# Row operations of two block inverses from VectorE to GpSimd, modulation rows from the recurrence to the projections

## The chip, the cores and the metric

The kernel runs on one core of a Trainium2 chip. The metric is the device time of one launch in microseconds. The engines are TensorE (PE in the profile, its weight loads PEld), VectorE (DVE), ScalarE (ACT), GpSimd (POOL) and the queue that issues most loads (SP).

## What is computed

Two blocks follow each other on 512 positions of width 1024, in float32. The first is modulated by a condition c, mixes the positions with a gated convolution and with a linear recurrence in both directions (after 256 positions of context), and ends in a convolutional feed-forward part. The second block (a gated linear recurrence, windowed attention, a gated feed-forward part) is not touched by the change. Cut to what matters:

```python
mod = silu(c) @ ada_w + ada_b                      # six parts of 1024: sh1, sc1, g1, sh2, sc2, g2
hx  = modulate(rms_norm(x, norm1_g), sh1, sc1)     # and the same for ctx
cb, cc, cx, r, k, v, w_lo, a_lo, g_lo = split_proj(hx @ w_in)
def step(S, inp):                                  # per head, 64 x 64, forward and reverse
    r_t, w_t, kk_t, b_t, v_t, k_t = inp
    sa = einsum("bhvk,bhk->bhv", S, kk_t)
    S = S * w_t - sa[..., None] * b_t + v_t[..., None] * k_t
    return S, einsum("bhvk,bhk->bhv", S, r_t)
y_conv = cb * shortconv1d(cc * cx, conv_a_w)
x = x + g1 * (concatenate([y_conv, y_rwkv]) @ w_out)
x = x + g2 * conv_ffn(modulate(rms_norm(x, norm2_g), sh2, sc2))
```

## The kernel before

**Products.** Large products run as three products of rounded parts (mm3): high by high, high by low, low by high. A weight piece of 128 x 512 is loaded (w), rounded by ScalarE (whi) and the rest is formed by VectorE, wlo = w - whi (split, L178 to L182; its argument `eng` can name another engine). wsplit does this for the pieces of a tile.

**Projections** (proj, some 60 to 261 us). 26 tiles of w_in come in a fixed order of code: 24, 16 to 19, 12 to 15, then the preparation of the first pair of heads, the products for v, tile 25, and for j = 0 to 3 the tiles 4+j, 8+j and j, with steps of the second pair's preparation between. A tile's two pieces are k0 = 0 and k0 = 4.

**Recurrence** (rwkv, 261 to 545 us). It goes through four pairs of heads, called pair 0 to 3 here (j in the code), in four stages, each of twelve groups g of one chunk per direction. A group is a chain of small products c and copies by ScalarE (RU, S); VectorE masks the scores psc into AS. Ahead of its stage each pair needs prep(j): low-rank products pl, decay sums cs (scan), b, KB and KR for each direction, products pa into AK, and then inverse(j), which inverts the 24 triangular 64 x 64 blocks: transpose to U, 31 steps of two operations on 128 partitions (tmp = U x X, X = X - tmp) with n*w = (31-k)(k+1) elements per partition, at most 256, two transposes F1 and F2, and two rounds of small products, pt and po. VectorE does the 62 operations of each inverse:

```python
tv = tmp[:, 0:n * w].rearrange("p (a b) -> p a b", b=w)
nc.vector.tensor_tensor(out=tv, in0=U[...].to_broadcast(...), in1=X[...].to_broadcast(...), op=ALU.mult)
nc.vector.tensor_tensor(out=X[:, k + 1:32, 0:w], in0=X[:, k + 1:32, 0:w], in1=tv, op=ALU.subtract)
```

inverse(0) runs beside the projections, inverse(1) in stage 0, inverse(2) in stage 1 and inverse(3) in stage 2. At the end of a stage GpSimd forms vt, rk and ys, and grs for the stage's normalisation.

**Modulation, second part** (ada12, L525 to L542). The parts of mod from g1 on come from 32 rows: each is a load of 128 x 1024 values (adaw) and one VectorE operation, a product with cb summed along the row (L539). The results go into self.mod, which is first read after the recurrence. The rows are taken from `todo`, the list of side work from which each group takes steps; after stage 1 it holds splits(), ada12() and first(), the last of which loads and splits the first two pieces of w_out, whose products px follow stage 3.

**Order.** The framework's scheduler orders each engine's stream ahead of time, by priorities that stage() sets (base + PK x g for the chain, plus PF for side work) and by its own model of durations. On the chip each engine takes its stream in order and waits for semaphores.

Of the kernel before, what the change touches and what calls it, by code (L numbers as in the profile page):

```python
# [10 lines left out]
F32 = mybir.dt.float32  # L11
# [3 lines left out]
ALU = mybir.AluOpType  # L15
# [3 lines left out]
P = 128  # L19
# [103 lines left out]
class K:  # L123
# [175 lines left out]
    def proj(self):  # L299
        nc, A, r1, p0 = self.nc, self.A, self.r1, self.p0  # L300
# [27 lines left out]
        acc = self.t3("acc", "sg")  # L328
# [13 lines left out]
        hc = [t[:, i, :] for tag, n in (("KB10", 6), ("KB11", 6), ("KR10", 5)) for t in [self.pp.tile([P, n, NC_], F32R, tag=tag, name="hc", bufs=1)] for i in range(n)]  # L342
        hhi = [[None] * KD, hc[:KD]]
        hlo = [[None] * KD, hc[KD:2 * KD]]
        piece = lambda u, k0: self.wsplit(A["win"][u][:, k0:k0 + 4], 4, P)
        ahead = {(24, k0): piece(24, k0) for k0 in (0, 4)}
        G = self.pp.tile([P, KD, 2], F32, tag="bo", name="G", bufs=2)
        for kc in range(KD):
# [12 lines left out]
                    nc.vector.scalar_tensor_tensor(out=hlo[i][kc], in0=xT[i][kc], scalar=sh, in1=hhi[i][kc].bitcast(F32), op0=ALU.add, op1=ALU.subtract)  # L361
        nc.gpsimd.memset(self.AK, 0.0)

        def tile_of(u, x=True, c=True):
            ws = [ahead.pop((u, k0), None) or piece(u, k0) for k0 in (0, 4)]
            w = lambda k: ws[k // 4](k % 4)
            out = []
            for on, i, n in ((x, 0, NX), (c, 1, NC_)):
                if on:
                    pm = self.psmm(n)  # L370
                    self.mm3(pm, [(*w(k), hhi[i][k], hlo[i][k]) for k in range(KD)])
                    out.append(pm)
            return out
# [80 lines left out]
        for j in range(4):  # L454
            t = self.zx[j]
            pcc, = tile_of(4 + j, c=False)
            nc.scalar.activation(out=t, in_=pcc, func=AF.Copy)
            pcx, = tile_of(8 + j, c=False)
            u = r1.tile([P, NX + 2], F32, tag="u", name="u", bufs=1)
            nc.gpsimd.memset(u[:, 0:1], 0.0)  # L460
            nc.gpsimd.memset(u[:, NX + 1:NX + 2], 0.0)
            nc.vector.tensor_tensor(out=u[:, 1:NX + 1], in0=t, in1=pcx, op=ALU.mult)
            nc.scalar.activation(out=t, in_=u[:, 0:NX], func=AF.Copy, scale=self.v("conva", j))
            for i in (1, 2):
                nc.vector.scalar_tensor_tensor(out=t, in0=u[:, i:i + NX], scalar=self.v("conva", 4 * i + j), in1=t, op0=ALU.mult, op1=ALU.add)
            pcb, = tile_of(j, c=False)
            nc.vector.tensor_tensor(out=t, in0=t, in1=pcb, op=ALU.mult)
            for _ in range(self.RC):
                next(self.todo, None)


    def consts(self):
# [5 lines left out]
    def rwkv(self, es, ep):  # L478
# [9 lines left out]
        for j in range(4):  # L488
            if j < 2:
                todo = chain(todo, self.prep(j + 2))  # L490
            gn = self.stage(j, self.S[j], todo, self.RB[j], gn)
            if j == 1:
                for _ in todo:
                    pass
                ep.close()
                self.wp = self.pool(es, "wp", side="right")
                self.mmbufs, self.axbufs, self.wbufs, self.wsbufs = 6, 2, 3, 4
                pa = self.pool(self.ea, "pmix", side="right")
                self.ahi = [pa.tile([P, NX], F32R, name=f"ahi{i}") for i in range(8)]
                self.alo = [pa.tile([P, NX], F32R, name=f"alo{i}") for i in range(8)]  # L500
                todo = chain(self.splits(), self.ada12(), self.first())
                self.e3 = es.enter_context(ExitStack())
                self.psa = self.psum(self.e3, "psa", side="right")
        for _ in todo:
# [20 lines left out]
    def ada12(self):  # L525

        nc, wp = self.nc, self.wp
        tags = [("w", self.wbufs), ("whi", self.wsbufs), ("wlo", self.wsbufs)]
        cb, sb = (wp.tile([P, 1024], F32, tag=tags[i][0], name="cb", bufs=tags[i][1]) for i in (1, 2))
        nc.sync.dma_start(out=cb, in_=self.A["cb"])  # L530
        nc.scalar.activation(out=sb, in_=cb, func=AF.Tanh, scale=0.5)
        nc.vector.tensor_scalar(out=sb, in0=sb, scalar1=0.5, scalar2=0.5, op0=ALU.mult, op1=ALU.add)
# [1 line left out]
        acc = wp.tile([P, 32], F32, name="adacc")  # L534
        for n in range(32):
            yield
            w, t = (wp.tile([P, 1024], F32, tag=tags[i][0], name="adaw", bufs=tags[i][1]) for i in (0, 2))
            nc.sync.dma_start(out=w, in_=self.A["adat"][n])
            nc.vector.scalar_tensor_tensor(out=t, in0=w, scalar=1.0, in1=cb, op0=ALU.mult, op1=ALU.mult, accum_out=acc[:, n:n + 1])  # L539
            if n in (7, 23, 31):  # L540
                a = 0 if n == 7 else 8 if n == 23 else 24
                nc.vector.tensor_tensor(out=self.mod[:, 16 + a:17 + n, 0], in0=acc[:, a:n + 1], in1=self.v("ada_b", 16 + a, n + 1 - a), op=ALU.add)  # L542
# [107 lines left out]
    def inverse(self, j):  # L650
# [12 lines left out]
        nc.vector.transpose(out=U, in_=AK[:, :, 0:32].rearrange("p n i -> p i n"))  # L663
        nc.gpsimd.memset(X, 0.0)
        nc.gpsimd.memset(X.rearrange("p a b -> p (a b)")[:, ::33], 1.0)
        for k in range(31):
            if k % 4 == 0:
                yield
            n, w = 31 - k, k + 1
            tv = tmp[:, 0:n * w].rearrange("p (a b) -> p a b", b=w)  # L670
            nc.vector.tensor_tensor(out=tv, in0=U[:, k + 1:32, k:k + 1].to_broadcast([P, n, w]), in1=X[:, k:k + 1, 0:w].to_broadcast([P, n, w]), op=ALU.mult)
            nc.vector.tensor_tensor(out=X[:, k + 1:32, 0:w], in0=X[:, k + 1:32, 0:w], in1=tv, op=ALU.subtract)
        F1, F2 = big("F1"), big("F2")
        nc.vector.transpose(out=F1.rearrange("p n i -> p i n"), in_=X)
        nc.vector.transpose(out=F2.rearrange("p n j -> p j n"), in_=X.rearrange("p i j -> p j i"))
# [721 lines left out]
```

## Time and profile before

| | |
|---|---|
| Median of three runs | 1590.84 us (1588.16 to 1595.9) |
| The profiled execution | 1591.34 us |
| Its span in the trace | 1589.5 us |
| TensorE busy | 1498.6 us, 94% |
| VectorE busy | 999.9 us, 63% |
| ScalarE busy | 632.7 us, 40% |
| GpSimd busy | 121.7 us, 8% |
| Projections / recurrence | about 60 to 261 / 261 to 545 us |

Times of a trace count from the start of the span; what the execution has beyond its span is 1.8 us. A matmul's busy time overlaps that of the next one. An idle time ahead of an instruction is put down to the event that ended it.

### The profile page before, as it was taken

How to read it: one execution, taken by the hardware profiler on the slowest of the kernel's cores; microseconds unless marked ns; L12 is line 12 of the kernel's file. 1: busy time of each engine (PE TensorE's matmuls, PEld its weight loads, DVE VectorE, ACT ScalarE, POOL GpSimd, SP SyncE). 2: the span in 40 equal slices, each digit the busy share in tenths (PEclk: the TensorE clock that was granted, in tenths of full speed). 3: DMA queues.
4: the chain of work that ended last, by engine and by line, in shares of the span. 5: the costliest groups of instructions: out<-in, count | busy, mean ns of one | idle time of the engine just before them, and what ended most of it. 6: DMA issues, size and time to landing. Idle time of an engine off the chain costs nothing. (4 is left out here: it accounts for less than half of the span.)

```text
span 1589.5 us, 28932 instructions
## 1 busy us (share of the span) xinstructions
PE 1498.6 (94%) x12062; PEld 1228.9 (77%) x12062; DVE 999.9 (63%) x1691; ACT 632.7 (40%) x1258; POOL 121.7 (8%) x141
## 2 busy tenths in 40 slices
PE   4899999989888999999999997999999999999998
PEld 2777787877777898888888875887677888888886
DVE  3436765777867669888863448588965555554221
ACT  3524343555453334333332325335554333333122
POOL 1111001020110000000000004121200000000000
PEclk9999898989999999999999998999999999999999
DMA  9243321010057613223323322211112222233221
GB/s 339 87 156 104 100 89 60 4 45 5 15 197 258 214 40 119 94 93 101 98 83 100 96 93 70 80 54 54 36 59 93 93 93 93 93 94 106 93 92 54
DMA packets 62179, 152.83 MB, mean 96 GB/s; under 512 B 12640, under 2 KB 14432, under 8 KB 62048
## 3 DMA queue, kind: packets, MB, share of 16 engines
q1 hardware_dynamic: 58016, 143.95, 27.9%
q10 hardware_dynamic: 4032, 7.04, 1.3%
q8 instruction: 94, 1.54, 0.4%
q14 instruction: 37, 0.30, 0.1%
HBM read 143.10 MB, written 7.86 MB: 95 GB/s over the span
## 5 line engine op out<-in xcount | busy, mean ns | idle before, releaser
L181 ACT ACTIVATE whi<-w 128x1024 fp32r<-128x1024 f32 (+2 forms) x220 | 208.7, 950 | 448.2 <-PE pm L170 333.3
L182 DVE TENSOR_TENSOR wlo<-w,whi 128x1024 fp32r<-128x1024 f32 (+2 forms) x212 | 229.9, 1086 | 201.3 <-ACT whi L181 195.3
L169 PE MATMUL pm<-ahi,whi 128*128 128x512 f32 (+1 forms) x624 | 236.4, 379 | 3.0 <-DVE sh L1080 2.6
L170 PE MATMUL pm<-alo,whi 128*128 128x512 f32 (+1 forms) x624 | 234.8, 376 | 0.0
L171 PE MATMUL pm<-ahi,wlo 128*128 128x512 f32 (+1 forms) x624 | 234.0, 375 | 0.0
L170 PE MATMUL pm<-al,whi 128*128 128x512 f32 x352 | 139.7, 397 | 0.0
L169 PE MATMUL pm<-ah,whi 128*128 128x512 f32 x352 | 139.2, 395 | 0.0
L171 PE MATMUL pm<-ah,wlo 128*128 128x512 f32 x352 | 139.2, 395 | 0.0
L169 PEld LDWEIGHTS pm<-ahi,whi 128*128 128x128 f32 x624 | 117.6, 189 | 24.2 <-ACT sh L1095 3.0
L171 PEld LDWEIGHTS pm<-ahi,wlo 128*128 128x128 f32 x624 | 117.6, 188 | 20.6 <-issue 0.7
L170 PEld LDWEIGHTS pm<-alo,whi 128*128 128x128 f32 x624 | 117.7, 189 | 20.3 <-issue 0.7
L953 DVE SCALAR_TENSOR_TENSOR cv<-pm,vec,cv 128x441 f32<-128x441 f32 (+2 forms) x176 | 121.1, 693 | 4.1
L170 PEld LDWEIGHTS pm<-al,whi 128*128 128x128 f32 x352 | 66.2, 188 | 16.1 <-issue 0.2
L171 PEld LDWEIGHTS pm<-ah,wlo 128*128 128x128 f32 x352 | 66.2, 188 | 16.1 <-issue 0.2
L169 PEld LDWEIGHTS pm<-ah,whi 128*128 128x128 f32 x352 | 66.2, 188 | 16.0
L171 PE MATMUL pm<-hhi,wlo 128*128 128x512 f32 x176 | 70.8, 402 | 2.7 <-DVE wlo L182 2.7
L169 PE MATMUL pm<-hhi,whi 128*128 128x512 f32 x176 | 71.4, 406 | 0.2 <-ACT whi L181 0.2
L170 PE MATMUL pm<-hlo,whi 128*128 128x512 f32 x176 | 70.6, 401 | 0.0
L169 PE MATMUL pd<-whi,gh 128*128 128x512 f32 x176 | 69.5, 395 | 0.0
L169 PE MATMUL pm<-hh,whi 128*128 128x512 f32 x176 | 69.3, 394 | 0.0
L170 PE MATMUL pm<-hl,whi 128*128 128x512 f32 x176 | 69.3, 394 | 0.0
L171 PE MATMUL pm<-hh,wlo 128*128 128x512 f32 x176 | 69.3, 394 | 0.0
(397 smaller groups left out, 3073.6 us busy)
## 6 DMA issues: line engine op xcount, KB each, us to landing
w<-in_fup SPq DMA_DIRECT2D x44, 512.0 KB, 3.7
adaw<-in_adat SPq DMA_DIRECT2D x32, 512.0 KB, 4.6
w<-in_win SPq DMA_DIRECT2D x44, 256.0 KB, 2.9
w<-in_wg SPq DMA_DIRECT2D x22, 512.0 KB, 3.6
w<-in_wu SPq DMA_DIRECT2D x22, 512.0 KB, 3.6
w<-in_wd SPq DMA_DIRECT2D x22, 512.0 KB, 3.7
w<-in_win SPq DMA_DIRECT2D x18, 512.0 KB, 3.5
w<-in_wout SPq DMA_DIRECT2D x16, 512.0 KB, 3.8
```

Of the source, the lines that this page charges most:

```text
L169: nc.tensor.matmul(out, lh, rh, start=(first and i == 0), stop=False)
L170: nc.tensor.matmul(out, lh, rl, start=False, stop=False)
L171: nc.tensor.matmul(out, ll, rh, start=False, stop=(last and i == n - 1))
L181: self.nc.scalar.activation(out=hi, in_=src, func=AF.Copy)
L182: (eng or self.nc.vector).tensor_tensor(out=lo, in0=src, in1=hi.bitcast(F32), op=ALU.subtract)
L953: nc.vector.scalar_tensor_tensor(out=o, in0=p[:, ro[0] + dr:ro[1] + dr, co[0] + dc:co[1] + dc], scalar=w(i), in1=o, op0=ALU.mult, op1=ALU.add)
```

## The change

It has three parts. (1) The row operations of the inverses of pairs 2 and 3 are issued on GpSimd instead of VectorE. (2) The 32 modulation rows are taken in proj: each tile takes one row for 12 <= u < 25 and two otherwise, from two row buffers of their own, and the product is written over the loaded row; todo after stage 1 holds splits() and first() alone. (3) For the tiles 25 and 0 to 11, the second piece's low part is formed by GpSimd. Lines below L363 move down by seven to ten; L671 and L672 are L681 and L682 in the new kernel, the modulation row L539 is L548, pt L701.

```diff
-        piece = lambda u, k0: self.wsplit(A["win"][u][:, k0:k0 + 4], 4, P)
+        piece = lambda u, k0: self.wsplit(A["win"][u][:, k0:k0 + 4], 4, P, eng=nc.gpsimd if k0 and not 12 <= u < 25 else None)
...
+        ada = self.ada12()
+        def rows(n):
+            for _ in range(n):
+                next(ada, None)
         def tile_of(u, x=True, c=True):
+            rows(1 if 12 <= u < 25 else 2)
             ws = [ahead.pop((u, k0), None) or piece(u, k0) for k0 in (0, 4)]
...
             for _ in range(self.RC):
                 next(self.todo, None)
+        for _ in ada:
+            pass
...
-                todo = chain(self.splits(), self.ada12(), self.first())
+                todo = chain(self.splits(), self.first())
...
-        tags = [("w", self.wbufs), ("whi", self.wsbufs), ("wlo", self.wsbufs)]
-        cb, sb = (wp.tile([P, 1024], F32, tag=tags[i][0], name="cb", bufs=tags[i][1]) for i in (1, 2))
+        row = lambda name: wp.tile([P, 1024], F32, tag="row", name=name, bufs=2)
+        cb, sb = wp.tile([P, 1024], F32, name="cb"), row("sb")
...
-            w, t = (wp.tile([P, 1024], F32, tag=tags[i][0], name="adaw", bufs=tags[i][1]) for i in (0, 2))
+            w = row("adaw")
             nc.sync.dma_start(out=w, in_=self.A["adat"][n])
-            nc.vector.scalar_tensor_tensor(out=t, in0=w, scalar=1.0, in1=cb, op0=ALU.mult, op1=ALU.mult, accum_out=acc[:, n:n + 1])
+            nc.vector.scalar_tensor_tensor(out=w, in0=w, scalar=1.0, in1=cb, op0=ALU.mult, op1=ALU.mult, accum_out=acc[:, n:n + 1])
...
+        e = nc.vector if j < 2 else nc.gpsimd
         for k in range(31):
...
-            nc.vector.tensor_tensor(out=tv, in0=U[:, k + 1:32, k:k + 1].to_broadcast([P, n, w]), ...
-            nc.vector.tensor_tensor(out=X[:, k + 1:32, 0:w], in0=X[:, k + 1:32, 0:w], in1=tv, op=ALU.subtract)
+            e.tensor_tensor(out=tv, in0=U[:, k + 1:32, k:k + 1].to_broadcast([P, n, w]), ...
+            e.tensor_tensor(out=X[:, k + 1:32, 0:w], in0=X[:, k + 1:32, 0:w], in1=tv, op=ALU.subtract)
```

Three places of the built order. First TensorE, stage 1, around the products pt of the inverse of pair 2; the c rows are the chain's products, c_2377 and c_2378 its two directions. Before, about the chain's tenth group:

```order
L638 MATMUL c_2377<-RU_2372,zx 64x64 x2
L638 MATMUL pkt<-cst,KB_1646 64x64 x2
L638 MATMUL c_2378<-vt,AS_2369 64x64 x2
L638 MATMUL c_2378<-S_2376,KR_1649 64x64
L691 MATMUL pt<-F_3309,AK 32x32 x24
L638 MATMUL c_2377<-vt,kbt 64x64 x2
L638 MATMUL c_2377<-S_2375,cst 64x64 x2
L638 MATMUL c_2377<-RU_2372,kbt 64x64
L638 MATMUL pa<-KR_86,KB_84 64x64 x10
L691 MATMUL pt<-F_3309,AK 32x32 x24
```

After, where c_2483 and c_2484 are the two directions:

```order
L647 MATMUL c_2483<-vt,kbt 64x64 x2
L647 MATMUL c_2483<-S_2481,cst 64x64 x2
L647 MATMUL c_2483<-RU_2478,kbt 64x64 x2
L647 MATMUL c_2483<-vt,AS_2473 64x64
L701 MATMUL pt<-F_3415,AK 32x32 x24
L647 MATMUL c_2483<-vt,AS_2473 64x64
L647 MATMUL c_2483<-S_2481,KR_1680 64x64 x2
L647 MATMUL c_2484<-RU_2480,zx 64x64 x2
L647 MATMUL pkt<-cst,KB_1678 64x64 x2
L647 MATMUL pa<-KR_86,KB_84 64x64 x9
L701 MATMUL pt<-F_3415,AK 32x32 x24
```

These products now stand about the sixth group, four groups earlier; those of pair 3 move in the same way from behind the eighth group of stage 2 to its third.

Second VectorE, projections, the end of the inverse of pair 0. Before:

```order
L671 TENSOR_TENSOR tmp<-U,X 128x87
L672 TENSOR_TENSOR X<-X,tmp 128x3x29
L671 TENSOR_TENSOR tmp<-U,X 128x60
L672 TENSOR_TENSOR X<-X,tmp 128x2x30
L671 TENSOR_TENSOR tmp<-U,X 128x31
L672 TENSOR_TENSOR X<-X,tmp 128x31
L674 STREAM_TRANSPOSE F_1294<-X 128x32x32
L675 STREAM_TRANSPOSE F_1295<-X 128x32x32
L192 COPY XT_83<-F_1294 128x768
L192 COPY XT_83<-F_1295 128x768
```

After:

```order
L682 TENSOR_TENSOR X<-X,tmp 128x5x27
L190 TENSOR_SCALAR sg<-sg,cst 128x12x64
L681 TENSOR_TENSOR tmp<-U,X 128x112
L600 SCALAR_TENSOR_TENSOR cs<-cst,sg 128x780
L682 TENSOR_TENSOR X<-X,tmp 128x4x28
L681 TENSOR_TENSOR tmp<-U,X 128x87
L619 SCALAR_TENSOR_TENSOR b_1924<-ta,kk 128x768
L682 TENSOR_TENSOR X<-X,tmp 128x3x29
L620 SCALAR_TENSOR_TENSOR KB_1678<-b_1924,sg 128x12x64
L681 TENSOR_TENSOR tmp<-U,X 128x60
L627 TENSOR_TENSOR KR_1680<-kk,cs 128x256
L682 TENSOR_TENSOR X<-X,tmp 128x2x30
```

The first operations of pair 1's prep (sg, cs, b, KB, KR) have moved between the last row operations, and a low part of the tiles stands there; further up, four modulation rows (L548) stand among the row operations of the same inverse, and 25 ahead of it.

Third VectorE, stage 1, the transposes F of the inverse of pair 2 and what follows. Before:

```order
L671 TENSOR_TENSOR tmp<-U,X 128x31
L672 TENSOR_TENSOR X<-X,tmp 128x31
L674 STREAM_TRANSPOSE F_3308<-X 128x32x32
L675 STREAM_TRANSPOSE F_3309<-X 128x32x32
L192 COPY XT_2364<-F_3308 128x768
L192 COPY XT_2364<-F_3309 128x768
L731 COPY_PREDICATED AS_2367<-cst,psc 128x384
L731 COPY_PREDICATED AS_2370<-cst,psc 128x384
L731 COPY_PREDICATED AS_2365<-cst,psc 128x2x64
L190 TENSOR_SCALAR sg<-sg,cst 128x12x64
```

After, with the row operations gone to GpSimd:

```order
L741 COPY_PREDICATED AS_2473<-cst,psc 128x384
L741 COPY_PREDICATED AS_2476<-cst,psc 128x384
L684 STREAM_TRANSPOSE F_3414<-X 128x32x32
L685 STREAM_TRANSPOSE F_3415<-X 128x32x32
L192 COPY XT_2470<-F_3414 128x768
L192 COPY XT_2470<-F_3415 128x768
L741 COPY_PREDICATED AS_2471<-cst,psc 128x384
L741 COPY_PREDICATED AS_2474<-cst,psc 128x384
L190 TENSOR_SCALAR sg<-sg,cst 128x12x64
L602 SCALAR_TENSOR_TENSOR cs<-cst,sg 128x780
```

The rest of pair 3's prep (sg, the scan of its second direction, b) still follows the transposes F, and no row operation stands ahead of them on this engine. On TensorE the pa products of pair 3's second direction, which need it, still follow pt. The first products px, which stood behind stage 3, now begin in stage 2's last group.

## Rows read from the trace of the kernel before

**Rows 1.** The page's list of engines: busy us (share of span) x instructions.

```profile
PE 1498.6 (94%) x12062; PEld 1228.9 (77%) x12062; DVE 999.9 (63%) x1691; ACT 632.7 (40%) x1258; POOL 121.7 (8%) x141
```

**Rows 2.** Stretches: us, busy us of PE, PEld, DVE, ACT, POOL, PEclk, DMA share, GB/s.

```profile
152.00:187.00 35.00, 31.19 (x173) 24.88 (x172) 33.17 (x77) 9.91 (x17) 2.62 (x4) 0.99 0.39 112
187.00:200.00 13.00, 12.65 (x216) 10.43 (x211) 3.18 (x5) 7.31 (x15) 1.57 (x4) 0.62 0.20 63
465.00:500.00 35.00, 31.49 (x770) 27.04 (x768) 27.04 (x50) 15.88 (x66) 3.20 (x3) 1.00 0.74 247
500.00:520.00 20.00, 16.34 (x350) 14.34 (x350) 14.50 (x26) 7.94 (x32) 1.04 (x1) 0.86 0.80 272
```

**Rows 3.** Waits, 250 to 560 us: engine, line, waited for: us, times, longest.

```profile
PE pt L691 <- DVE F L675: 2.9, 3, 1.3
PE c L638 <- DVE AS L731: 5.9, 6, 1.5
PEld c L638 <- ACT RU L759: 8.3, 18, 2.8
```

**Rows 4.** Timeline of DVE: start us, us, engine, line, operation, shapes [idle before <-releaser].

```profile
184.25 1.88 DVE L675 STREAM_TRANSPOSE F<-X 128x1024 f32<-128x1024 f32 x1
331.42 0.29 DVE L671 TENSOR_TENSOR tmp<-U,X 128x31 f32<-128x31 f32 x1
376.78 1.95 DVE L675 STREAM_TRANSPOSE F<-X 128x1024 f32<-128x1024 f32 x1
398.43 1.94 DVE L663 STREAM_TRANSPOSE U<-AK 128x1024 f32<-128x1024 f32 x1 [2.10 <-POOL AK L660]
```

**Rows 5.** Timeline of ACT (S) and POOL (vt), recurrence, in order of time.

```profile
366.23 0.31 ACT L769 ACTIVATE S<-c,pc 128x64 f32<-128x64 f32 x1 [0.96 <-PE c L638]
400.02 1.04 POOL L789 TENSOR_TENSOR vt<-vt,bo 128x512 f32<-128x512 f32 x1 [0.39 <-PE c L638]
411.41 0.31 ACT L769 ACTIVATE S<-c,pc 128x64 f32<-128x64 f32 x1 [0.58 <-PE c L638]
432.28 0.31 ACT L769 ACTIVATE S<-c,pc 128x64 f32<-128x64 f32 x1 [0.96 <-PE c L638]
464.29 1.04 POOL L789 TENSOR_TENSOR vt<-vt,bo 128x512 f32<-128x512 f32 x1 [23.34 <-issue]
517.17 1.04 POOL L789 TENSOR_TENSOR vt<-vt,bo 128x512 f32<-128x512 f32 x1 [38.74 <-PE c L638]
```

**Rows 6.** Groups, DVE, 331 to 376 us: shapes xcount | busy us, mean ns | idle.

```profile
L672 DVE TENSOR_TENSOR X<-X,tmp 128x31 f32<-128x31 f32 (+15 forms) x31 | 11.5, 371 | 0.7
```

**Rows 7.** Groups of POOL by shape, whole span, same columns.

```profile
L823 POOL TENSOR_TENSOR grs<-gv,mhalf 128x8 f32<-128x8 f32 x4 | 6.6, 1648 | 26.2 <-DVE gv L820 16.0 <-DMA adaw<-in_adat 10.2
L359 POOL TENSOR_TENSOR hc<-KB,hc 128x256 fp32r<-128x256 f32 x8 | 6.6, 832 | 14.8 <-ACT KB L358 14.8
L789 POOL TENSOR_TENSOR vt<-vt,bo 128x512 f32<-128x512 f32 x4 | 4.2, 1042 | 62.5 <-PE c L638 39.1 <-issue 23.3
L808 POOL TENSOR_TENSOR ys<-Y 128x512 f32<-128x512 f32 x3 | 3.8, 1262 | 0.0
L601 POOL COPY pc<-cs 128x12 f32<-128x12 f32 x8 | 3.0, 372 | 92.1 <-ACT cs L597 92.1
```

**Rows 8.** Timeline of DVE and POOL at the third inverse's start.

```profile
331.62 1.26 POOL L563 TENSOR_TENSOR rk<-rt,kt 128x512 f32<-128x512 f32 x1
331.74 1.21 DVE L672 TENSOR_TENSOR X<-X,tmp 128x31 f32<-128x31 f32 x1
```

**Rows 9.** Timeline of DVE: one modulation row, stage 2.

```profile
451.91 1.23 DVE L539 SCALAR_TENSOR_TENSOR adaw<-adaw,cb 128x1024 f32<-128x1024 f32 x1
```

**Rows 10.** Groups of PE, 519 to 545 us: first of three such.

```profile
L169 PE MATMUL px<-ahi,whi 128*128 128x512 f32 x16 | 7.4, 476 | 1.3 <-ACT ahi L181 1.3
```

**Rows 11.** Timeline of DVE: prep of pair 3, second direction.

```profile
388.82 1.78 DVE L593 TENSOR_TENSOR_SCAN cs<-cst,sg 128x780 f32<-128x780 f32 x1
391.04 0.95 DVE L610 SCALAR_TENSOR_TENSOR b<-ta,kk 128x768 f32<-128x768 f32 x1
```

More of the change, by code (lines that the diff above doesn't have):

```diff
@@ L670, in inverse @@
             tv = tmp[:, 0:n * w].rearrange("p (a b) -> p a b", b=w)
-            nc.vector.tensor_tensor(out=tv, in0=U[:, k + 1:32, k:k + 1].to_broadcast([P, n, w]), in1=X[:, k:k + 1, 0:w].to_broadcast([P, n, w]), op=ALU.mult)
-            nc.vector.tensor_tensor(out=X[:, k + 1:32, 0:w], in0=X[:, k + 1:32, 0:w], in1=tv, op=ALU.subtract)
+            e.tensor_tensor(out=tv, in0=U[:, k + 1:32, k:k + 1].to_broadcast([P, n, w]), in1=X[:, k:k + 1, 0:w].to_broadcast([P, n, w]), op=ALU.mult)
+            e.tensor_tensor(out=X[:, k + 1:32, 0:w], in0=X[:, k + 1:32, 0:w], in1=tv, op=ALU.subtract)
         F1, F2 = big("F1"), big("F2")
```

## The prediction

> **What bounds the kernel now.** The list of engines gives TensorE 1498.6 of 1589.5 us [rows 1], so the first question of any stretch is whether TensorE works or waits there. The table of stretches answers it. The change touches two places. Late in the projections (152 to 187 us) TensorE and VectorE are both nearly full, 31.19 and 33.17 of 35 us, and right after it, at 187 to 200, the granted clock is 0.62, the lower of TensorE's two levels for most of the stretch [rows 2]. In the recurrence (261 to 545 us) TensorE waits in small pieces: in the last stage, 465 to 520 us, it works 31.49 of 35 and 16.34 of 20 us, 7.2 us idle [rows 2]. The list of waits says for whom: the two inverses there cost TensorE only 2.9 us in three pieces at pt, VectorE's AS copies 5.9 us, ScalarE's RU 8.3 us [rows 3]. So VectorE's row operations are long but almost hidden; what an edit can win in the recurrence is a few us of AS waits, and the holes.
>
> The timeline shows how the inverse of pair 2 lies: its first row operation at 331.42, its second F transpose from 376.78, so ready at 378.73, and then 19.7 us until the U of pair 3 starts at 398.43 [rows 4]. Those 19.7 us are a chain that starts at pt: pt and po, then the low-rank products, sg, scan, b, KB, KR of pair 3's second direction, pa, and AK. In the changed order the same work still stands behind pt on TensorE and behind F on VectorE. Stages 1 and 2 end at 400.02 and 464.29, where vt is written [rows 5]. ScalarE's S rows place pt's new positions: half-way through the sixth of stage 1's twelve groups (TensorE there at 366) and in the third group of stage 2 (411) [rows 5].
>
> **Row operations on GpSimd.** Each of the two inverses gives 62 operations, 2 x 5456 elements per partition. VectorE did the second half of each pair in 11.5 us for 31, so about 23 us for 62 [rows 6]. The trace has no such small operation on GpSimd. The nearest rows: a subtraction of 256 elements takes 0.832 us, an addition of 512 1.262, one with a broadcast operand 1.042, a copy of 12 elements 0.372 [rows 7]. From 256 to 512 that is 1.68 ns an element over a fixed 0.40 us, and the copy of 12 says the same of the fixed part. So 62 x 0.40 = 24.8, 5456 x 1.68 = 9.2 for the subtractions, 5456 x (1042 - 400)/512 = 6.8 for the broadcast products: 41 us. No operation has more than 256 elements, so 62 x 0.832 = 51.5 us is an upper end; VectorE's own 23 us is the lower end that I work with, 18 us if GpSimd's small operations cost still less. I take 41, since both rows near the small sizes agree on the fixed part.
>
> Inverse of pair 2: GpSimd is free after vt at about 331.7. 41 us of its own; rk, ys, grs and pc stand in between, 1.26 + 1.26 + 1.65 + 0.37 = 4.5 us [rows 7]; and 4 us for collisions (0 to 8). For these: at 331.74 a 31-element VectorE operation took 1.21 us while GpSimd's rk ran from 331.62 [rows 8], where its twin at 331.42 took 0.29 [rows 4]. So the two engines do exclude each other; no row shows GpSimd as the one that waits, but none shows it working for long beside VectorE, whose other two-input work there is some 8 us. Then two F transposes, 3.9 us: ready at 385.1, where TensorE stands before pt since 366. A new wait of 19 us. From this place to the end of stage 1 TensorE had 400 - 366 = 34 us of work, 1.3 of it the old pt wait: stage 1 ends at 417.8.
>
> The Trainium skill, "SBUF — State Buffer", "SBUF: two separate sides", calls the shared port pair an exclusive lock, in which whichever of a VectorE operation with two SBUF inputs and a GpSimd operation starts first blocks the other for the whole instruction; rows 8 agree for one direction. By the rule in both directions the collisions are at their upper end and the sum would be 6 us higher, by the rows alone 6 us lower.
>
> Inverse of pair 3: U starts 19.7 us after 385.1, at 404.8, and takes 2. Then 41 us, vt, ys and grs in between 4, collisions 2, F 3.9: ready at 457.7. TensorE comes to pt at 417.8 + 11 = 428.8: a second wait, 29 us. Left of stage 2 behind this place are 464.3 - 411 = 53.3 us, less the old pt wait, RU's 2.8 (ScalarE's tanh of cb is gone from there) and some 2 of AS: 47. Stage 2 ends at 504.7, 40.4 later than before. VectorE is freed of 46 us here, but nobody waits for that: the AS waits that it ends are 5.9 us in all [rows 3] and disappear into the longer ones.
>
> **Modulation rows out of stages 2 and 3, first wout products in.** A row costs VectorE 1.23 us [rows 9] and a 512 KB load. Stage 3 ran from 464.29 to 517.17, 4.4 us for each of twelve groups, against (432.28 - 411.41)/5 = 4.17 from the third to the eighth group of stage 2, ahead of the rows [rows 5]: -3. The 48 products px stood behind stage 3; three groups like the one of 7.4 us overlap in pairs, some 10.5 us [rows 10], and now stand from stage 2's last group on. They fit into holes that measured 7.2 us: -7 (0 to -10).
>
> **Modulation rows and low parts in the projections.** 25 of the 32 rows stand ahead of the inverse of pair 0, in front of work with which VectorE has room, and their loads meet a DMA share of 0.39, where 0.80 is carried at 500 us [rows 2]: nothing for these, 1.5 for VectorE being later at pa. Inside this inverse, where VectorE has 1.8 us free, there now stand four rows, 4.9, and the head of pair 1's prep: the scan 1.78, sg and three more at most like b, 0.95, and a third of one [rows 11], 5.9 together. Three low parts go, each with half a row's elements, 1.8. Sum +9 until F. GpSimd's low parts at 1.3 us can hold a VectorE operation as in rows 8: 0 to 5, taken as 2. About 2 us more TensorE work stands ahead of pt. So pt, which TensorE waited for until 186.13 [rows 4], stands 11 us later and finds 2 of them filled, and TensorE, otherwise full, waits out the rest; with the 1.5 that is +10 (4 to 17). The end 4 is that the rows fall into gaps; 17 is all collisions and a second stretch at the lower clock like that of 187 to 200.
>
> **Sum**: 40.4 - 3 - 7 + 10 = +40 against the profiled execution of 1591.3, which is 0.5 above the median of 1590.84. Forecast 1631, its own range 1612 to 1650 (5 us more or less of each GpSimd series is 10 in the end, since the second series starts from the end of the first).
>
> **Rivals.** *GpSimd's small operations cost as much as its 256-element one.* 51.5 us each: F of pair 2 at 395.6, U of pair 3 at 415.3, F at 478.7, stage 2 to 525.7, sum +61: 1653. For it: the operations have two- and three-dimensional patterns with short rows, the rows of GpSimd are mostly long runs; against it, the copy of 12 at 0.372. *About the same.* At VectorE's price, 23 us, F of pair 2 is ready before TensorE's 366, U of pair 3 at about 386 and F at 418, stage 2 ends at 465.5, and -3, -7 and +10 cancel: 1592. It needs 0.37 us an operation, just the fixed part. *Faster.* 18 us (0.29 us an operation): stage 2 ends at 460.5, and the projections give only +4 because the rows fall into gaps: 1591 - 4 - 10 + 4 = 1581. It decides at under some 20 us a series together with a projections term under 5. For it: the rows hold no two-operand operation of GpSimd under 256 elements but the powers; against it, 18 us over 62 operations leaves nothing beside 0.29 us each, and the 12-element copy alone takes 0.372. That the change does not do what it says is out: the order shows 124 row operations on GpSimd.
>
> **How the numbers follow.** About 0.5%, 8 us, is what a measurement can tell from no change. Forecast 0.55, dear operations 0.20, about the same 0.14, faster 0.11. The range 1586 to 1658 leaves out most of the faster case and the upper part of the dear one. Slower by more than 0.5%: 0.75, within 0.14, faster 0.11.
>
> **What would show it.** Right: GpSimd's row operations at a mean of 0.6 to 0.75 us, some 40 to 46 us from first to last; waits of TensorE at pt for F of about 19 and 29 us; in the projections a wait of about 10 us ahead of pt near 190 to 200; modulation rows all before 215 us; px inside stage 3. Wrong: a mean under 0.4 us, pt waits of a few us, or stage 2 ending near 465. If the waits are there but stage 2 ends much before 500, the work behind pt was shorter than read; if the second wait is no longer than the first, U of pair 3 did not hang on pt.

## The result

The changed kernel takes 1631.95 us (median of four runs, 1625.93 to 1637.68) against 1589.5 (the median of four runs of the kernel before, one more than in the table above): a ratio of 1.0262, 95% interval 1.0212 to 1.0312. The forecast was 1631. The profiled execution took 1631.23 us with a span of 1629.4, 39.9 more than the span before.

The list of engines of the page after, to be read against [rows 1]: TensorE's work is the same, VectorE lost 39.5 us, GpSimd gained 93, and TensorE's idle time grew from 90.9 to 126.3 us.

```profile
PE 1503.1 (92%) x12062; PEld 1235.6 (76%) x12062; DVE 960.4 (59%) x1554; ACT 633.9 (39%) x1258; POOL 214.5 (13%) x278
```

Where the 39.9 us lie is read from GpSimd's vt, which is written when a stage's last chunk is done (stages 0, 2 and 3; that of stage 1 stands behind other work in GpSimd's queue and tells nothing). The vt of stage 0 before, and the timeline after, to be read against it and [rows 5]:

```profile
330.62 1.04 POOL L789 TENSOR_TENSOR vt<-vt,bo 128x512 f32<-128x512 f32 x1
```

```profile
341.69 1.04 POOL L799 TENSOR_TENSOR vt<-vt,bo 128x512 f32<-128x512 f32 x1 [0.30 <-PE c L647]
449.21 1.04 POOL L799 TENSOR_TENSOR vt<-vt,bo 128x512 f32<-128x512 f32 x1
517.98 1.04 POOL L799 TENSOR_TENSOR vt<-vt,bo 128x512 f32<-128x512 f32 x1 [46.94 <-issue]
568.19 1.04 POOL L799 TENSOR_TENSOR vt<-vt,bo 128x512 f32<-128x512 f32 x1 [42.91 <-PE c L647]
```

| Part of the span | Before | After | Difference | Term of the sum |
|---|---|---|---|---|
| to the end of stage 0 | 330.6 | 341.7 | +11.1 | +10 |
| stages 1 and 2 | 133.7 | 176.3 | +42.6 | +40.4 |
| stage 3 | 52.9 | 50.2 | -2.7 | -3 |
| behind stage 3 | 1072.3 | 1061.2 | -11.1 | -7 |

In the changed kernel without its row operations (e4 below) stages 1 and 2 last 136.3 us, so 40.0 of the 42.6 come with the row operations. TensorE's busy time there is 126.25 us after and 121.24 in e4, at mean granted clocks of 0.78 and 0.97. So some 35 us of the 40 are idle time, and 5 are the same kind of work done at a lower clock, a term that the forecast did not have.

TensorE's waits after, 330 to 520 us (engine, line, waited for: us in all, times, longest), and the table of stretches of the recurrence (columns as in [rows 2]):

```profile
PE pt L701 <- DVE F L685: 22.6, 2, 13.6
PE pv L647 <- POOL vt L799: 15.8, 2, 15.5
PE pa L647 <- DVE KB L620: 7.4, 1, 7.4
```

```profile
350.00:380.00 30.00, 22.27 (x401) 19.04 (x398) 13.69 (x16) 12.74 (x39) 27.54 (x36) 0.74 0.05 15
380.00:400.00 20.00, 6.55 (x161) 6.19 (x165) 5.01 (x5) 3.46 (x9) 10.23 (x24) 0.57 0.00 1
400.00:450.00 50.00, 34.03 (x818) 29.10 (x818) 14.18 (x19) 20.84 (x71) 26.50 (x47) 0.81 0.01 4
450.00:480.00 30.00, 19.93 (x498) 18.82 (x499) 10.43 (x16) 10.97 (x33) 15.25 (x28) 0.64 0.20 67
```

From 350 to 400 us GpSimd is the fullest engine. Between 380 and 400 TensorE works 6.55 of 20 us at a granted clock of 0.57, and from 400 to 480 it works about two thirds of the time. Four waits make up 45.4 us. The timeline of TensorE shows them in order, each with the idle time ahead of it:

```profile
368.69 0.37 PE L647 MATMUL pa<-KR,KB 64*64 64x64 f32 x1 [7.38 <-DVE KB L620]
393.45 1.49 PE L701 MATMUL pt<-F,AK 32*32 32x32 f32 x48 [13.56 <-DVE F L685]
450.31 0.79 PE L647 MATMUL pv<-cst,vt 64*64 64x64 f32 x9 [15.50 <-POOL vt L799]
468.50 1.49 PE L701 MATMUL pt<-F,AK 32*32 32x32 f32 x48 [8.99 <-DVE F L685]
```

Two of the four have another name than the wait for F that was forecast, but the same source. The first: GpSimd's grs stands in the middle of the row operations; VectorE's yc waits 7.3 us for it, and b, KR and KB of pair 3, for which TensorE's pa waits, are queued behind yc on VectorE. GpSimd's and VectorE's timeline:

```profile
362.34 1.66 POOL L833 TENSOR_TENSOR grs<-gv,mhalf 128x8 f32<-128x8 f32 x1
```

```profile
364.03 1.12 DVE L835 TENSOR_TENSOR yc<-yc,grs 128x512 f32<-128x512 f32 x1 [7.34 <-POOL grs L833]
365.07 1.43 DVE L619 SCALAR_TENSOR_TENSOR b<-ta,kk 128x768 f32<-128x768 f32 x1
367.20 1.43 DVE L620 SCALAR_TENSOR_TENSOR KB<-b,sg 128x768 f32<-128x768 f32 x1
```

The third wait: vt of stage 1 stands behind 41 row operations of pair 3, so that TensorE's pv, placed early in stage 2, waits until 450.31.

The series themselves, first and last row operation of either, one operation of 192 elements in both and the largest, and then the second F and the U around the second series (GpSimd's, then VectorE's timeline):

```profile
342.69 0.25 POOL L681 TENSOR_TENSOR tmp<-U,X 128x31 f32<-128x31 f32 x1
353.39 1.94 POOL L682 TENSOR_TENSOR X<-X,tmp 128x192 f32<-128x192 f32 x1
389.45 0.25 POOL L682 TENSOR_TENSOR X<-X,tmp 128x31 f32<-128x31 f32 x1
423.33 0.26 POOL L681 TENSOR_TENSOR tmp<-U,X 128x31 f32<-128x31 f32 x1 [0.91 <-DVE U L672]
430.64 0.59 POOL L682 TENSOR_TENSOR X<-X,tmp 128x192 f32<-128x192 f32 x1
442.02 0.73 POOL L682 TENSOR_TENSOR X<-X,tmp 128x256 f32<-128x256 f32 x1
464.48 0.25 POOL L682 TENSOR_TENSOR X<-X,tmp 128x31 f32<-128x31 f32 x1
```

```profile
391.50 1.89 DVE L685 STREAM_TRANSPOSE F<-X 128x1024 f32<-128x1024 f32 x1
421.23 1.96 DVE L672 STREAM_TRANSPOSE U<-AK 128x1024 f32<-128x1024 f32 x1 [1.64 <-POOL AK L669]
466.54 1.92 DVE L685 STREAM_TRANSPOSE F<-X 128x1024 f32<-128x1024 f32 x1
```

The first lasts 47.0 us, 5.2 of them other work (rk 1.26, ys 1.27, grs 1.66, pc 0.92, a memset 0.12); the second 41.4, less vt, ys and grs, 4.0: 37.4 us of its own, against 41.8 in the first. In the second nearly nothing of VectorE stands in the way. The 4.4 us of difference are read as collisions: the operations that grew in the first series stand beside VectorE's two-input operations, like that of 353.39 beside the scan (last section).

In the projections the wait has another name as well. TensorE does not come to pt first; it waits for a weight's high part on ScalarE (ScalarE's, then TensorE's timeline, and VectorE's second F of pair 0):

```profile
196.73 0.84 ACT L605 ACTIVATE sg<-cs 128x768 f32<-128x768 f32 x1 [3.71 <-DVE cs L600]
197.61 0.85 ACT L606 ACTIVATE cs<-cs 128x780 f32<-128x780 f32 x1
198.37 0.61 ACT L181 ACTIVATE whi<-w 128x512 fp32r<-128x512 f32 x1
```

```profile
199.03 0.79 PE L169 MATMUL pm<-hhi,whi 128*128 128x512 f32 x1 [6.74 <-ACT whi L181]
```

```profile
205.07 2.13 DVE L685 STREAM_TRANSPOSE F<-X 128x1024 f32<-128x1024 f32 x1
```

ScalarE's exponential needs VectorE's scan, which stands between the last row operations of pair 0 and starts at 194.84; whi stands behind it in ScalarE's queue.

### The profile page after: what moved, and what is told of

It reads as the page before. It is cut to its first block, busy times and chain, and to the rows that moved or that the text cites. A ratio compares the mean times of both kernels' runs of the same rounds, so it can differ in the third digit from the quotient of the medians.

```text
span 1629.4 us, 28921 instructions
## 1 busy us (share of the span) xinstructions
PE 1503.1 (92%) x12062; PEld 1235.6 (76%) x12062; DVE 960.4 (59%) x1554; ACT 633.9 (39%) x1258; POOL 214.5 (13%) x278
## 5 line engine op out<-in xcount | busy, mean ns | idle before, releaser
L182 DVE TENSOR_TENSOR wlo<-w,whi 128x1024 fp32r<-128x1024 f32 (+2 forms) x199 | 220.7, 1110 | 169.6 <-ACT whi L181 167.7
L169 PEld LDWEIGHTS pm<-ah,whi 128*128 128x128 f32 x352 | 66.1, 188 | 15.5
L741 DVE COPY_PREDICATED AS<-cst,psc 128x384 f32<-128x384 int32 (+1 forms) x48 | 23.3, 490 | 79.6 <-PE psc L647 79.3
L170 PE MATMUL pd<-wlo,gh 128*128 128x512 f32 x176 | 69.5, 395 | 0.0
L171 PE MATMUL pd<-whi,gl 128*128 128x512 f32 x176 | 69.5, 395 | 0.0
```

The costliest lines, as they stand in the source:

```text
L169: nc.tensor.matmul(out, lh, rh, start=(first and i == 0), stop=False)
L170: nc.tensor.matmul(out, lh, rl, start=False, stop=False)
L171: nc.tensor.matmul(out, ll, rh, start=False, stop=(last and i == n - 1))
L182: (eng or self.nc.vector).tensor_tensor(out=lo, in0=src, in1=hi.bitcast(F32), op=ALU.subtract)
L741: nc.vector.copy_predicated(A[:, :, 0:N], m.unsqueeze(1).to_broadcast([P, 2, N]), ps)
```

## The experiments

Ratios are to the kernel before, with 95% intervals, each against runs on the same chip. "Stages 1, 2" is the time from vt of stage 0 to vt of stage 2 in the run's trace: 133.7 us before, 176.3 after.

| Run | Ratio | Interval | Median us | Stages 1, 2 |
|---|---|---|---|---|
| row operations alone (e1) | 1.0266 | 1.0230 to 1.0303 | 1631.54 | 175.4 |
| modulation rows alone (e2) | 1.0007 | 0.9988 to 1.0026 | 1589.97 | 137.3 |
| changed, without row operations (e4) | 1.0013 | 0.9996 to 1.0030 | 1590.32 | 136.3 |
| changed, without low parts (e5) | 1.0245 | 1.0218 to 1.0272 | 1627.92 | 176.9 |
| vt and ys on VectorE (e6) | 1.0245 | 1.0220 to 1.0271 | 1624.42 | 171.5 |
| pair 3 alone on GpSimd (e7) | 1.0117 | 1.0072 to 1.0161 | 1608.22 | 156.3 |
| pair 2 alone on GpSimd (e8) | 1.0106 | 1.0084 to 1.0128 | 1602.52 | 154.7 |
| both on GpSimd, pt late (e9c) | 1.0233 | 1.0200 to 1.0266 | 1622.51 | 167.2 |
| pair 2 alone, pt late (e9) | 1.0060 | 1.0036 to 1.0084 | 1598.46 | 147.8 |
| products twice (e10) | 1.0403 | 1.0379 to 1.0428 | 1650.02 | 202.0 |
| wout ahead of the rows (e11) | 1.0037 | 1.0021 to 1.0052 | 1594.75 | 137.9 |
| all rows early (e12) | 1.0120 | 1.0099 to 1.0141 | 1607.79 | 137.9 |

### Which part costs the time

The row operations alone, on the kernel before:

```diff
+        e = nc.vector if j < 2 else nc.gpsimd
         for k in range(31):
...
-            nc.vector.tensor_tensor(out=tv, ...
-            nc.vector.tensor_tensor(out=X[:, k + 1:32, 0:w], ...
+            e.tensor_tensor(out=tv, ...
+            e.tensor_tensor(out=X[:, k + 1:32, 0:w], ...
```

> The first part alone: the kernel before with the row operations of the inverses of pairs 2 and 3 on GpSimd, modulation rows and low parts where they were. Theory (the GpSimd series are late and TensorE waits for each): the projections end as before, GpSimd's series last 41 to 47 us each, TensorE waits some 21 us for the first and some 24 us for the second, the end comes 35 to 45 us later than before, 1625 to 1635 us. Rival (the loss of the changed kernel sits in the projections and in collisions with the moved rows): under 1605 us.

The modulation rows alone (the changed kernel with `e = nc.vector` and without `eng=` in piece), and the changed kernel without its row operations (`e = nc.vector` alone):

> The second part alone: modulation rows in the projections, row operations and low parts on VectorE as before. Theory: the projections lose 7 to 11 us, and the recurrence and the first wout products gain 12 to 16, so 1582 to 1590 us. Rival (the first wout products move because VectorE is free of row operations, not because the rows are gone): no gain behind the projections, 1596 to 1602 us.

> The changed kernel without its first part: row operations of all inverses on VectorE, modulation rows and half of the low parts as changed. Theory: within 3 us of the second part alone, a little slower because GpSimd's low parts of 1.3 us hold VectorE at a few places: 1584 to 1592 us. Rival (half of the low parts on GpSimd free VectorE where it is full): 3 to 6 us faster than the second part alone.

The changed kernel without its low parts:

```diff
-        piece = lambda u, k0: self.wsplit(..., 4, P, eng=nc.gpsimd if k0 and not 12 <= u < 25 else None)
+        piece = lambda u, k0: self.wsplit(..., 4, P)
```

> The changed kernel without its third part: all low parts on VectorE. Theory (the low parts matter little): within 3 us of the changed kernel, 1627 to 1634 us. Rival (they cost the projections most of their 11 us): 1621 to 1626 us.

The row operations alone measure 1.0266, the whole change 1.0262: the first part is the whole loss. The other two parts together are 1.0013, no difference that can be told from none. For the second part alone the theory's gain is not there: 1589.97 is the upper end of its range, with a median of 1588.81 before on that chip. Its trace does show the two halves, a later end of stage 3 (520.94 against 517.17) and 11 us less behind it (1061.1 against 1072.3), but the execution that was profiled, 1583.77, is near the low end of its ten runs (1583.71 to 1595.08). Of the third part nothing can be measured in either pair (e2 against e4, e5 against the changed kernel). TensorE's longest waits of e1 in 330 to 600 us are those of the changed kernel, with rows and low parts where they were:

```profile
PE pt L692 <- DVE F L676: 22.8, 2, 13.8
PE pv L638 <- POOL vt L790: 16.5, 4, 15.5
PE pa L638 <- DVE KB L611: 8.8, 1, 8.8
```

### Is vt's place in GpSimd's queue the cause

The wait of 15.5 us for vt was not forecast, so vt and ys were given to VectorE:

```diff
-        nc.gpsimd.tensor_tensor(out=bv, in0=bv, in1=wide(bo), op=ALU.mult)
+        nc.vector.tensor_tensor(out=bv, in0=bv, in1=wide(bo), op=ALU.mult)
...
-        (nc.vector if j == 3 else nc.gpsimd).tensor_tensor(out=ys, ...
+        nc.vector.tensor_tensor(out=ys, ...
```

> The changed kernel with vt and ys of the stages' normalisation on VectorE instead of GpSimd, so that they no longer stand behind GpSimd's row operations; grs stays. Theory (the end of GpSimd's second series ends the wait, the wait for vt lies inside it): the 15.5 us wait at pv goes, the wait at pt for F grows from 9 to some 20 us, and only GpSimd's 2.3 us and a little more are won: 1626 to 1631 us. Rival (vt's place in GpSimd's queue is itself what is late): 1614 to 1620 us.

TensorE's waits of this run, 330 to 600 us:

```profile
PE pt L701 <- DVE F L685: 35.5, 2, 22.4
PE pa L647 <- DVE KB L620: 13.0, 1, 13.0
```

The wait for vt is gone, and that for F grew from 9.0 to 22.4: what ended the wait before was the series, and vt lay inside it. The wait for KB grew from 7.4 to 13.0, behind grs once more: VectorE comes to yc earlier, and yc waits 11.8 us for grs, which kept its place in the middle of the series. Stages 1 and 2 fell by 4.8 us, the time by 1.0262 - 1.0245, some 3 us (the intervals overlap). By its waits that is the theory's case. The median of 1624.42 lies between the two ranges, but on a chip on which the kernel before takes 1586.4; the ratio, put on 1589.5, gives 1628. No run here takes grs off GpSimd.

### Do the two series add up or compound

Pair 2 alone and pair 3 alone on GpSimd (`e = nc.gpsimd if j == 2 else nc.vector`, and `e = nc.vector if j < 3 else nc.gpsimd`):

> The changed kernel with the row operations of pair 2 alone on GpSimd, those of pair 3 on VectorE. Theory (each series costs its own wait, and the second starts from the first's end): the waits at pa and pt of stage 1 stay, 7 and 14 us, those of stage 2 are gone; pair 3's pt stands in the sixth group of stage 2 and VectorE's series is ready about there: 1606 to 1616 us. Rival (TensorE's second wait only takes over the first's delay, one series costs as much as two): 1625 to 1632 us.

> The changed kernel with the row operations of pair 3 alone on GpSimd, those of pair 2 on VectorE. In the built order pair 3's pt stands in the sixth group of stage 2. Theory (together the two cost more than their sum, since the second starts from the first's end; the loss of both is 2.6%, that of pair 2 alone 1.1%): U of pair 3 some 15 us earlier than in the changed kernel, F ready 49 us after it, a wait of 15 to 20 us, ratio 1.007 to 1.012. Rival (the second series alone causes what pair 2 alone doesn't): 1.015 or more.

TensorE's waits of e8 and of e7, 330 to 600 us:

```profile
PE pt L701 <- DVE F L685: 14.7, 2, 13.6
PE pa L647 <- DVE KB L620: 7.4, 1, 7.4
```

```profile
PE pt L701 <- DVE F L685: 15.0, 2, 14.5
PE c L647 <- DVE AS L741: 7.1, 2, 6.1
```

Against the changed kernel without row operations (136.3 us), stages 1 and 2 are 18.4 us longer with pair 2, 20.0 with pair 3 and 40.0 with both. So in the traces the two add up, within 2 us, and e7's "together the two cost more than their sum" is not borne out there. The medians (0.9% and 1.0% above e4, both together 2.5%) would leave room for some 8 us more, but cannot show them, with an interval of 0.9% on e7. Of e7's forecasts, the ratio of 1.0117 is inside the range and the wait of 14.5 us just under it. In e7 pair 3's U starts at 409.57, counted from stage 0's end 10 us earlier than in the changed kernel, so the first series does push the second; but pt then stands three groups later in the order than with both, and behind F are 39.8 us of stage 2 instead of 49.5. The 6.1 us wait for AS in e7 has grs in it once more: VectorE's yc (424.82) waits 6.39 us for it, and AS is queued behind yc.

Each product twice, which makes either series some 18 us longer (first to last row operation 65.0 and 59.3 us against 47.0 and 41.4):

```diff
-            e.tensor_tensor(out=tv, ...
+            for _ in range(1 if j < 2 else 2):
+                e.tensor_tensor(out=tv, ...
```

> The changed kernel with each product of GpSimd's row operations done twice, 31 more operations in either series, 16 to 17 us. In the built order pt of pair 2 moves to the eighth group of stage 1 and that of pair 3 to the sixth of stage 2. Theory (F sets the end, and the second series starts from the end of the first): twice the added time, 30 to 36 us: 1660 to 1668 us. Rival (the two series do not hang together, or TensorE's other work covers a part): 15 to 20 us, 1646 to 1653 us.

Measured are 22 us by the ratios (1.0403 - 1.0262 of 1589) and 25.7 in stages 1 and 2: between the theory's 30 to 36 and the rival's 15 to 20, so neither came out. (The median of 1650.02 is in the rival's range, but the kernel before is 3 us faster on this chip.) The second F does come 34 us later, with both additions in it (502.18 against 466.54, less 1.7 at stage 0's end), but the order puts its pt at the sixth group instead of the third, and what is behind it takes 41.3 us instead of 49.5.

### The place or the price

Two readings are left: TensorE loses the time because pt stands too early in its order (the place), or because the series is too long wherever pt stands (the price). They were put to the test by leaving all row operations on GpSimd and moving pt. The F transposes of pair 2 get a product by zero with the chain's state S0 ahead of them, written into an element that is zero, in the ninth group; and the first steps of pair 3's prep, which pt does not hold, are taken meanwhile (cut; self.at is the stage and group, self.p3 the prep of pair 3):

```diff
+        if j == 2:
+            n3 = 0
+            while self.at < (1, 9):
+                if n3 < 6 and self.at[0] == 1:
+                    next(self.p3)
+                    n3 += 1
+                yield
+            nc.vector.tensor_scalar(out=X[:, 0, 31:32], in0=self.S0[0][:, 0:1], scalar1=0.0, scalar2=None, op0=ALU.mult)
         F1, F2 = big("F1"), big("F2")
```

> The changed kernel, all 124 row operations on GpSimd as there, but the F transposes of pair 2 tied to the ninth group of stage 1, so that in the built order its pt stands in the tenth group instead of the sixth and pair 3's pt in the eighth of stage 2 instead of the third. Theory of the place (TensorE loses the time because pt stands in its order long before GpSimd is done): the series are as long as before, but TensorE has the chain to do meanwhile; waits at pt of some 3 and 6 to 10 us, 1595 to 1612 us. Rival, the price (a series of 42 us is too long wherever pt stands, since AK, U and the next series hang on it): 1622 us or more.

> Only pair 2's row operations on GpSimd, and its pt in the tenth group of stage 1 instead of the sixth (the other run with pair 2 alone on GpSimd measured 1.0106 of before). Theory (a single series costs only where its pt stands): stage 1 lasts some 73 us instead of 94, pair 3's series on VectorE is ready before its pt in the eleventh group of stage 2, and the ratio falls to 1.000 to 1.005. Rival (the later AK and U of pair 3 give the loss back in stage 2): 1.009 or more.

Both kernels have this edit; e9 has pair 3 on VectorE. GpSimd's vt and VectorE's U and second F of pair 3 in e9c, and TensorE's waits there:

```profile
337.24 1.04 POOL L809 TENSOR_TENSOR vt<-vt,bo 128x512 f32<-128x512 f32 x1 [0.41 <-PE c L648]
410.27 1.04 POOL L809 TENSOR_TENSOR vt<-vt,bo 128x512 f32<-128x512 f32 x1 [9.70 <-issue]
504.42 1.04 POOL L809 TENSOR_TENSOR vt<-vt,bo 128x512 f32<-128x512 f32 x1 [29.97 <-issue]
```

```profile
429.12 1.95 DVE L673 STREAM_TRANSPOSE U<-AK 128x1024 f32<-128x1024 f32 x1 [1.56 <-POOL AK L670]
469.95 1.91 DVE L694 STREAM_TRANSPOSE F<-X 128x1024 f32<-128x1024 f32 x1
```

```profile
PE pt L710 <- DVE F L694: 22.7, 2, 21.3
PE c L648 <- ACT RU L779: 8.8, 1, 8.8
```

Stage 1 lasts 73.0 us here, 94.2 in e8 (from vt to vt), 69.3 in e4, and the wait at its pt is 1.4 us instead of 13.6: for the first wait at pt the place was nearly the whole cost, and a later place takes it away. The 8.8 us for RU are the wait behind grs again: ScalarE's RU stands behind its copy of ta, which waits 8.8 us for VectorE's b, and b stands behind yc, which waits 8.7 us for grs. But pair 3's U now starts 91.9 us behind the vt of stage 0 instead of 79.5, since AK is free only after pt and the rest of pair 3's prep follows it, and stage 2 lasts 94.2 us, with a single wait of 21.3 at the second pt. The ratio of 1.0233 lies on the rival's side, and its interval overlaps that of the changed kernel.

With pair 3 on VectorE the late place is worth 1.0106 - 1.0060, some 7 us, and 1.0060 falls between the theory's range and the rival's. TensorE's waits for F (330 to 600 us) fall from 14.7 to 2.1 us in all; the largest left is the one for RU, 9.0. Stage 1 is 22.3 us shorter than in e8 (71.9 against 94.2) and stage 2 15.5 longer (75.9 against 60.4), but these two are not waits alone: work moved too, 1294 of TensorE's matmul records instead of 1484 in stage 1 and 1542 instead of 1356 in stage 2.

So for one series the place decides the wait at pt, and what stays of the loss is led by grs. For two it moves the wait from the first pt to the second: U to F, pt, the next U and its F are one chain, and 37 to 42 us of GpSimd twice make it longer than the work that TensorE has for it. That last step is argued from the order of events in e9c. Whether a pair 3 whose AK did not wait for pt of pair 2, or a grs on another engine, would change it wasn't tried.

### Can the second part be had for less

Two attempts at a kernel faster than both. The first changes one line of the kernel before; the second is e2 with all rows ahead of pair 0's inverse:

```diff
-                todo = chain(self.splits(), self.ada12(), self.first())
+                todo = chain(self.splits(), self.first(), self.ada12())
```

```diff
-            rows(1 if 12 <= u < 25 else 2)
+            rows(4 if 12 <= u < 25 else 0)
```

> The kernel before with one line changed: the side work after stage 1 takes the first two pieces of w_out ahead of the modulation rows instead of behind them. Theory (the gain behind the projections is px moved into TensorE's holes, and needs no row moved): px stand in stages 2 and 3, 4 to 10 us faster than before, ratio 0.994 to 0.9975. Rival (px between the chain's products delay the chain by as much): 0.998 to 1.002.

> The second part alone with all 32 modulation rows ahead of the inverse of pair 0: four for each of the first nine tiles, none later; row operations and low parts on VectorE. Theory (the rows cost the projections only inside that inverse, where VectorE is full): the projections end within 2 us of before and the gain behind them stays, ratio 0.992 to 0.997. Rival (the rows' loads, 512 KB each, hold up the weight loads in the same queue early on): the projections lose 4 us or more, ratio 0.998 to 1.004.

Neither is faster. With px ahead of the rows the ratio is 1.0037, just past the rival's range: px do stand in stages 2 and 3, but from the end of stage 0 to that of stage 3 the trace shows 188.8 us against 186.6, and behind stage 3 it gains 2.5. From the end of stage 0 on the two traces take the same, 1258.6 and 1258.9 us. The difference lies before that (336.59 against 330.62), in a part of the program that the edit does not touch, 3.5 us of it in the last stretch of stage 0 at a granted clock of 0.73 against 0.92. Why the median is some 6 us longer is open. With all rows early TensorE waits for rk (waits of 60 to 152 us, then GpSimd's timeline):

```profile
PE pb L647 <- POOL rk L572: 15.6, 1, 15.6
```

```profile
140.13 1.53 POOL L572 TENSOR_TENSOR rk<-rt,kt 128x512 f32<-128x512 f32 x1 [28.76 <-DMA lw<-in_lora]
```

rk began at 120.43 before. Its inputs kt and rt go out to memory and come back through SP's queue. From 60 us on, 26 loads of 512 KB stand there ahead of rt's, which SP issues at 135.68 instead of 106.13, and SP itself waits 40.5 us (60 to 152) for VectorE to free one of the two row buffers. This is the rival's mechanism, in the loads of pair 0 rather than of the weights; but 1.0120 is well above the rival's range too. Of all kernels run none is faster than the kernel before.

## Why the prediction came out right

**The price of GpSimd's operations.** Forecast 41 us of its own for either series and 4 and 2 us of collisions; measured 41.8 with collisions and 37.4 with almost none. Two errors in it partly cancel. The fixed part was read too high: the 0.372 us of the 12-element copy [rows 7] is a mean over eight, and in that trace they range from 0.20 (at 278.11) to 0.64 us (at 209.90); a row operation of 31 elements takes 0.25. The shortest of the group was the price, the mean wasn't: the longest (0.64, 0.54, 0.46) stand beside VectorE's two-input operations. By the rows after, 0.19 us and 0.08 between two operations instead of 0.40, that is an estimated 8 us too much over 62. The price per element was read too low, 1.68 and 1.25 ns against some 2.1 for a subtraction and 1.7 for a product (0.64 us for 256 elements, at 441.30): an estimated 5 us too little. The collisions of the first series were read right by the half-way value. A row operation takes 0.61 us in the mean in the first series and 0.53 in the second, where 0.6 to 0.75 was named as the sign. The dear rival (51.5 us) and the cheap one (18) are out.

**The first wait.** Forecast 19 us at pt; measured 13.6 there and 7.4 at pa, 21.0 in all. That grs would hold VectorE, and with it KB, was not seen: the step counted what grs adds to GpSimd's queue and did not ask who waits for grs. So 2 us of difference hide a wait that the forecast did not have.

**The second wait.** F was forecast for 457.7, which with the 11.1 us by which stage 0 ends later is 468.8; it was ready at 468.5. This is luck: it hides errors that cancel. U came 27.8 us after the first F, not 19.7 (F ends at 393.4, U starts at 421.23), and the series was 3.6 us cheaper, with nothing of the 2 us of collisions, while F had come 2.8 us earlier than forecast. The 19.7 us were taken over from before; but in the new order more of the chain's work stands between pt and AK, and TensorE is full there, at a lower clock (before and after, columns as in [rows 2]):

```profile
378.70:398.40 19.70, 16.98 (x516) 14.58 (x516) 10.10 (x16) 14.38 (x39) 4.12 (x7) 1.00 0.02 4
```

```profile
393.40:421.20 27.80, 27.34 (x632) 23.73 (x634) 11.79 (x17) 16.68 (x48) 3.77 (x7) 0.76 0.02 5
```

The wait was put at 29 us; it is 15.5 at pv and 9.0 at pt, 24.5. That vt would be late for TensorE was missed; by e6 it cost some 3 to 5 us at most, since F ends later. Behind pt the forecast had 47 us, and 49.5 were left. The 40.4 us of stages 1 and 2 are 40.0 by e4.

**Counting a series twice.** The rule that 5 us more in each series are 10 in the end was too strong. By e7 and e8 two series cost what each costs alone, about 18 to 20 us; by e10 18 us more in each are 22 to 26 in the end. The order that the scheduler builds moves pt with the series, and the forecast had held it in its place.

**Behind stage 2.** -3 for stage 3 was -2.7. Behind stage 3 it is -11.1, not -7: the 48 products px left their place nearly altogether, some 10.5 us by [rows 10]. The holes took most of them, not all: without row operations (e4) stages 1 and 2 are 2.6 us longer than before and stage 3 2.4 shorter, so the two terms together are -10.9, against -10.

**The projections.** +10 was +11.1, but this pair of traces does not show it so closely. 2.6 us stand already at the first px of the v tiles (134.4 before, 137.0 after), as the starts of two executions differ by some us. 3.4 us more stand in the last stretch of stage 0, from pt of pair 1 to vt, which is the chain in both (before and after):

```profile
308.84:330.62 21.78, 18.39 (x511) 15.63 (x512) 10.80 (x15) 14.85 (x42) 5.05 (x11) 0.92 0.19 63
```

```profile
316.52:341.69 25.17, 22.41 (x506) 19.39 (x508) 11.04 (x15) 15.15 (x42) 5.05 (x11) 0.73 0.17 55
```

The granted clock there, 0.92 or 0.73, does not go with the rows: e1, with the rows in their old place, takes 25.21 us at 0.73, and e2, with the rows moved, 21.72 at 0.92. Some 5 us are left for the rows and low parts in this pair. The medians say more: e4 is 1.5 us slower than the kernel before on its chip, with 10.9 us less from the end of stage 0 on, which would leave some 12. So the size of this term is known to several us only, and that +10 came so close is in part luck.

The mechanism was named half. The forecast had F 9 us later, 11 with collisions, and TensorE waiting for it at pt. F was 21 us later (207.2 against 186.13), and at pt TensorE no longer waited: whi and F both came late, whi first in TensorE's order. The prep of pair 1 between the row operations does hold TensorE, but by ScalarE, whose queue has whi behind the exponential that waits for the scan, 6.7 us. Three of the rows came behind F, the last at 218.56, not before 215. That the rows cost here what they win later, as +10, -3 and -7 had it, agrees with e4's 1.0013.

The lock rule of the Trainium skill, "SBUF — State Buffer", "SBUF: two separate sides", was weighed as 6 us up or down; the trace after shows it in the direction that no row read from before had: GpSimd as the one that waits (last section). Its upper end, 8 us in the first series, was not reached: GpSimd lost 4.4 us, and in the same stretch VectorE was held as well.

## What to carry to other kernels

An operation moved to a free engine is not free when it is a serial chain on which the full engine waits: compare the chain's length there with the time from its input to its consumer, and ask what else is queued on that engine (here grs and vt) and who waits for that. Where a scheduler with its own prices builds the order, moving a series also moves its consumer (here pt went from the tenth to the sixth group), so look where the consumer stands in the built order before pricing the wait. And a mean over a group may contain operations that were held: its shortest was nearest the price here.

## What the hardware showed that was not expected

GpSimd waits for VectorE too. While VectorE's scan ran, a row operation that takes 0.59 us undisturbed (430.64, above) took 1.94 us (353.39). VectorE's timeline:

```profile
353.18 1.78 DVE L600 TENSOR_TENSOR_SCAN cs<-cst,sg 128x780 f32<-128x780 f32 x1
```

It began behind the scan and ended 0.37 us after it: 353.18 + 1.78 = 354.96, and 353.39 + 1.94 = 355.33. So it was held through most of the scan; spans on GpSimd are rough, but e9c shows the same, 1.95 us (348.91) beside a scan of 1.87 (348.61). The trace before held this already, in rows that were not read: the copy of 12 elements took 0.64 us (209.90) beside VectorE's wlo (209.79, 0.69 us), and 0.20 (278.11) beside a masking copy. VectorE's operations with two inputs grew likewise some 12 us later, b from 0.95 us [rows 11] to 1.43 (365.07, above).

GpSimd's small operations are cheaper than its larger ones let one expect: undisturbed subtractions take 0.25 us for 31 elements, 0.59 for 192, 0.73 for 256, which is about 2.1 ns an element over 0.18 us, with some 0.08 us between operations; products with broadcast operands take 0.64 for 256.
